# Other buffers for two scratch tiles, and two changes of order, in a kernel of two transformer blocks

## The chip, the cores and the metric

The kernel runs on one core of one Trainium2 chip. The metric is the device time of one execution in microseconds, the median of three runs. Engines are named as in the profile: PE is TensorE, ACT is ScalarE, DVE is VectorE, POOL is GpSimd, and SP is the engine whose queue issues nearly all DMAs.

## The reference, cut to what matters

One sequence of 512 tokens of width 1024 passes through two transformer blocks of float32 weights.

```python
# first block
h = rms_norm(x, ln_pre_mix); proj = h @ w_in          # 256 pool columns, q, k, v of 12 heads of 64
q, k = rope(q, pos), rope(k, pos)
mix = concat(multi_scale_pool(proj), dilated_attention(q, k, v)) @ w_out
x = x + rms_norm(mix, ln_post_mix)
f = (silu(h2 @ w_gate) * (h2 @ w_up)) @ w_down        # h2 = rms_norm(x, ...), inner width 2816
x = x + rms_norm(f, ln_post_ffn)
# second block
z = rms_norm_2(h, ln_mix) @ w_in                      # parts q1 q2 k1 k2 va | qf kf vf fg | qc kc vc
q1, q2, k1, k2, qf, kf, qc, kc = (rms_norm_2(each head, gain) for each part)
o_a = diff_attention(q1, q2, k1, k2, va, lam, ...)    # 4 heads: softmax(q1 k1) - lam * softmax(q2 k2)
o_b = forgetting_attention(qf, kf, vf, log_f)         # 6 heads, cumulated log of a forget gate as bias
o_c = chunk_attention(qc, kc, vc, rel_bias)           # 6 heads, relative bias
h = h + concat(o_a, o_b, o_c) @ w_out
h = h + conv_gated_mlp(rms_norm_2(h, ln_ffn), w_up, conv_w, conv_b, w_down)
h = h + (p @ w_ple_proj) * sigmoid(rms_norm_2(h, ln_ple) @ w_ple_gate)
```

## The kernel before

**Matmuls.** Every product with weights is made of three TensorE passes: hi times hi, hi times lo and lo times hi, where hi is a value rounded for TensorE and lo the rest. A projection with 256 output columns (`chunk`, L374 to L376) takes 96 matmuls: four token tiles, eight input slices, three passes. Two token tiles share a PSUM bank, so each projection has two halves, and a function `out_of` takes a half out of PSUM as soon as it is complete. The slabs of the output projections (`slab`, L188 to L190) have 512 columns and put 128 output features into one bank.

**Weights.** `wunit` (L151) requests 512 KB of weights by one DMA on SP (L159) into a landing buffer of the tag "raw", of which the pool `wts` holds four. ACT copies each half of it to a hi tile (L165), and DVE, or now and then POOL, subtracts to get the lo tile (L168). When both halves are converted the landing buffer is free. Hi and lo tiles have nine buffers each.

**Slots.** Other tiles come from tags with fixed counts (`SLOTS`: sixteen "h", six "z", eight "m" and so on). Buffers of a tag are handed out in the order in which the program asks for them, and a tile waits until the last readers of the buffer's tile before are done. PSUM has three banks for projections and head transposes, two for scores, two for transposed weights of the attention, and one for outputs.

**Order of the work.** The attention part of each block is written as a string of steps (`ORDER1`, `ORDER2`), which `play` calls one by one. Of block 2's letters these matter here: D makes the first two projections, P and a digit one more (all with a norm of each head); V and a letter one of the value projections VM, VA, VF and VC; T and a digit transposes a projection's result into heads (L318), evacuates them by ACT and DVE (L330 to L333) and moves halves between partitions by copies on SP (L420); S and two digits makes scores (L263, L264, then L267 and L113), W transposes the softmax (L285) and multiplies it with values (L293, L294); F is the decay of the forgetting heads (L976 and more copies on SP); O is an output slab made early from the heads that are done. A scheduler then turns the recorded program into one fixed order for each engine, which it may change against the string, where dependencies allow it.

**The four places of the change.** In block 1 `out_of` of `project` copies a projection into a z slot (L488), and the rotation uses a second z slot, `y` (POOL L493, L494, DVE L495 to L497). In block 2 `out_of` of `projected` copies the half into a z slot (ACT, L832), writes its square into a second one (ACT, L833), and DVE reduces the square to eight sums for each row (L835); Ln and Exp (both L113) and a few small steps on DVE make the factors that POOL applies. `ORDER2` has the steps D, VM, H, P3, T1, T0 at its start. `add_out` loops over the eight slabs of an output projection; for the first four of w_out2 (`short` is 4) only the part over the last two heads tiles is left, since the steps O made the rest.

Of the kernel before, what the change touches and what calls it, by code (L numbers as in the profile page):

```python
# [9 lines left out]
F32 = mybir.dt.float32  # L10
# [5 lines left out]
P = 128  # L16
S = 512
D = 1024
KD = D // P
# [4 lines left out]
WH = 524  # L24
# [10 lines left out]
    "W31 S40 V2 S41 T5 U0 w40 s50 U1 B W41 S51 W50 W51 "  # L35
)
ORDER2 = (
# [3 lines left out]
)  # L41
# [21 lines left out]
class Builder:  # L63
# [388 lines left out]
    def mix1(self):  # L452
        nc = self.nc
        io = self.io
        x, h = [], []
        early = self.units("w_qk1", 0)
        for k in range(KD):
            x.extend(self.load_x((k,)))
            h.append(self.split(x[k], self.col("ln_pre_mix", k), tag="h"))
            if k in (0, 4):  # L460
                early(k // 4)
        self.rest()
        rope = self.slot("m", F32, (P, 4, 96))
        nc.sync.dma_start(rope, io["rope"])
        nc.sync.dma_start(self.ident, io["ident"])
        acc = self.slot("m")
        for k in range(KD):
            self.square_acc(acc, x[k], k == 0, after=self.last)
        R = self.slot("m")
        rc = self.rstd_cols(acc)  # L470
        rot = self.slot("m", F32, (P, 4, 96))
        for t in range(4):
            nc.vector.tensor_scalar(rot[:, t], rope[:, t], rc[:, 2 * t:2 * t + 1], None, ALU.mult)
        tab = self.slot("m")
        nc.sync.dma_start(tab, io["tab_mult"])

        zs = {}
        ops = {}
        ps = {}
        outs = {}  # L480

        def project(i):
            zs[i] = []

            def out_of(t1, ps):
                t0 = t1 - 1
                z, y = self.slot("z"), self.slot("z")
                nc.scalar.activation(z, ps, AF.Copy)  # L488
                zv, yv = [a.rearrange("p (t h d) -> p t h d", t=2, d=64) for a in (z, y)]
                cs = rot[:, t0:t0 + 2, 0:64].unsqueeze(2).to_broadcast([P, 2, 4, 64])  # L490
                sn = rot[:, t0:t0 + 2, 64:96].unsqueeze(2).to_broadcast([P, 2, 4, 32])
                a, b = slice(0, 32), slice(32, 64)
                nc.gpsimd.tensor_tensor(yv[:, :, :, a], zv[:, :, :, b], sn, ALU.mult)  # L493
                nc.gpsimd.tensor_tensor(yv[:, :, :, b], zv[:, :, :, a], sn, ALU.mult)  # L494
                nc.vector.tensor_tensor(zv, zv, cs, ALU.mult)  # L495
                nc.vector.tensor_tensor(zv[:, :, :, a], zv[:, :, :, a], yv[:, :, :, a], ALU.subtract)
                nc.vector.tensor_tensor(zv[:, :, :, b], zv[:, :, :, b], yv[:, :, :, b], ALU.add)  # L497
                zs[i].append(z)
            self.chunk("w_qk1", int(i), h, 256, out_of, i == "0", early)

        def heads(i):
            ops[i] = self.to_heads(zs[i], -0.125, None)

        oT = [None] * 8
        vts = []

        def values(g):
            vt = self.v_tiles()
            vts.append(vt)
            self.chunk("w_v1", int(g), h, 256, lambda t, ps: self.put_v2(vt, t, ps, rc))  # L510

        def score(i, e, wide=False):
            ps[i + e] = self.scores(ops[i][int(e)], tab, wide)

        def weigh(i, e, wide=False):
            i, e, p = int(i), int(e), ps[i + e]
            if e == 0:
                outs[i] = self.slot("o")
            j = (2 * i + e) % 4
            self.weigh(p, [vts[i // 2][t][:, j, :] for t in range(4)], outs[i], e == 1, wide)  # L520
            if e == 1:
                oT[2 + i] = self.split(outs[i], tag="o")

        us = []
        get = self.units("w_u1")

        def pool_in(i):
            if i == "0":
                self.rstd_rows(acc, R)
            u = self.psum()  # L530
            self.slab(u, "w_u1", int(i), h, units=get)
            t = self.slot("z")
            nc.vector.tensor_tensor(t, u, R, ALU.mult)
            us.append(t)

        self.play(ORDER1, P=project, T=heads, V=values, S=score, W=weigh, U=pool_in,
                  B=lambda: self.pool_branch(us, oT))
        return self.post(oT, DONE1, "w_out", "ln_post_mix", "ln_pre_ffn", True)
# [249 lines left out]
    def mix2(self, h, rc):  # L788
# [30 lines left out]
        zs = {}  # L819
# [7 lines left out]
        def projected(i):  # L827
            out = zs[i] = []

            def out_of(t1, ps):  # L830
                z, sq = self.slot("z"), self.slot("z")
                nc.scalar.activation(z, ps, AF.Copy)  # L832
                nc.scalar.activation(sq, ps, AF.Square)  # L833
                st = self.small(8)
                nc.vector.tensor_reduce(st, sq.rearrange("p (h d) -> p h d", d=64), AX.X, ALU.add)  # L835
                four = lambda v: v[:, t1 - 1:t1 + 1].unsqueeze(2).to_broadcast([P, 2, 4])
                two = lambda v: v.rearrange("p (t h) -> p t h", h=4)
                nc.vector.tensor_tensor(two(st), two(st), four(r2), ALU.mult)
                y, w = self.small(8), self.small(8)
                self.act(y, st, AF.Ln, bias=self.eps, scale=1.0)  # L840
                self.act(y, y, AF.Exp, scale=-0.5)
                nc.vector.scalar_tensor_tensor(w, st, EPS, y, ALU.add, ALU.mult)
                nc.vector.scalar_tensor_tensor(w, w, -0.5, y, ALU.mult, ALU.mult)
                nc.vector.tensor_tensor(two(y), two(y), four(r1), ALU.mult)
                nc.vector.scalar_tensor_tensor(st, w, 1.5, y, ALU.add, ALU.mult)
                zv = z.rearrange("p (h d) -> p h d", d=64)
                nc.gpsimd.tensor_tensor(zv, zv, st.unsqueeze(2).to_broadcast([P, 8, 64]), ALU.mult)
                out.append(z)
            return out_of
# [88 lines left out]
        def early(m):  # L938
# [10 lines left out]
                  F=lambda: fr.extend(self.decay(gates)), G=self.ple)  # L949
# [45 lines left out]
    def add_out(self, a, wname, nname, order=None, tag="z", old=None, short=0):  # L995
        nc = self.nc
        get = self.units(wname)
        h = self.h_tiles()
        old = old or self.res
        getb = self.units(wname + "b")  # L1000
        for m in range(KD):
            ps = self.psum(True)
            hv = ((0, S),) if m < KD - 1 else ((0, 256), (256, S))
            if m < short:
                self.slab(ps, wname, m, a, order[KA2:], hv, getb)
            else:
                self.slab(ps, wname, m - short, a, order, hv, get)
            for c0, c1 in hv:
                c = slice(c0, c1)
                nc.vector.tensor_tensor(self.res[m][:, c], old[m][:, c], ps[:, c], ALU.add)  # L1010
                self.split(self.res[m], self.col(nname, m), *h[m], cols=c)
        return h, self.stats(True, tag)
# [196 lines left out]
```

## Time and profile before

| what | value |
|---|---|
| runs, us | 1325.31, 1321.66, 1320.98; median 1321.66 |
| profiled execution, us | 1321.43 |
| its span, us | 1319.6 |
| TensorE's mean granted clock | 0.998 of full speed |
| busy, us | PE 1287.4, DVE 926.1, ACT 713.9, POOL 141.2 |

The span is the part of the execution from the first instruction to the last. A busy time counts an engine's instructions, and TensorE's matmuls overlap, so that a start-to-start distance is read from a stretch without idle time, by its length and its count. The idle time that stands in brackets behind an instruction is that of its engine just before it, with the instruction that released it. The rows that are read closely stand in a section of their own below.

### The profile page before, as it was taken

The numbers are of one execution on the slowest core, as the hardware profiler recorded it, in microseconds if no ns is written. First come the engines' busy times: TensorE is split into PE (matmuls) and PEld (weight loads), VectorE is DVE, ScalarE is ACT, GpSimd is POOL, SyncE is SP. The second block draws the span as 40 slices with busy tenths as digits, with TensorE's granted clock in tenths as the row PEclk, the third lists the DMA queues.
The fourth block names the chain that finished last, engine by engine and source line by source line (L and its number), as shares of the span: only waits on it lengthen the run. The fifth ranks groups of instructions, "written<-read, shape, count | busy, mean of one in ns | idle before, by whom it ended". The sixth has DMA issues, their size and how long they took to land.

```text
span 1319.6 us, 21593 instructions
## 1 busy us (share of the span) xinstructions
PE 1287.4 (98%) x7990; PEld 1145.5 (87%) x7990; DVE 926.1 (70%) x1949; ACT 713.9 (54%) x1446; POOL 141.2 (11%) x185
## 2 busy tenths in 40 slices
PE   9899989999999999999999999899999999999998
PEld 9899878988999988898899999779888888888887
DVE  7777884899999833249788878657977777633354
ACT  6466645564666633247676777645544444522241
POOL 1223220000000000000232333420000000000000
PEclk9999999999999999999999999999999999999999
DMA  7421433421333442227335443323322222322211
GB/s 253 125 68 50 112 104 104 144 96 63 118 119 102 148 156 96 96 104 241 106 90 133 135 118 101 103 104 121 128 96 96 96 97 96 104 96 96 96 49 64
DMA packets 51114, 146.00 MB, mean 111 GB/s; under 512 B 6496, under 2 KB 7392, under 8 KB 51008
## 3 DMA queue, kind: packets, MB, share of 16 engines
q1 hardware_dynamic: 51008, 144.62, 33.8%
q8 instruction: 63, 1.03, 0.3%
q14 instruction: 43, 0.35, 0.1%
HBM read 124.47 MB, written 8.39 MB: 101 GB/s over the span
## 4 chain that ended last, share of the span: by engine, by line
PE 88%; DVE 6%; ACT 2%; issue 2%; DMA 1%; POOL 1%; SPq 0%; DVEq 0%; POOLq 0%; ACTq 0%
PE p L188 22%; PE p L190 22%; PE p L189 22%; PE p L374 5%; PE p L376 5%; PE p L375 5%; PE p L285 2%; PE p L294 1%; PE p L264 1%; PE p L263 1%; PE p L293 1%; DVE sp L267 1%; DVE wl L168 1%; PE p L318 1%; PE p L399 1%
## 5 line engine op out<-in xcount | busy, mean ns | idle before, releaser
L165 ACT ACTIVATE wh<-wr 128x512 fp32r<-128x512 f32 x357 | 222.0, 630 | 296.3 <-PE p L189 261.1
L168 DVE TENSOR_TENSOR wl<-wr,wh 128x512 fp32r<-128x512 f32 x345 | 246.5, 722 | 189.0 <-ACT wh L165 177.7
L188 PE MATMUL p<-sh,wh 128*128 128x512 f32 (+1 forms) x736 | 249.0, 343 | 2.4 <-DVE sv L416 2.4
L189 PE MATMUL p<-sh,wh 128*128 128x512 f32 (+1 forms) x736 | 250.6, 343 | 0.0
L190 PE MATMUL p<-sh,wl 128*128 128x512 f32 (+1 forms) x736 | 248.2, 343 | 0.0
L374 PE MATMUL p<-wh,sh 128*128 128x256 f32 (+1 forms) x672 | 190.2, 284 | 4.1 <-ACT sz L488 1.4
L375 PE MATMUL p<-wl,sh 128*128 128x256 f32 (+1 forms) x672 | 190.0, 283 | 0.2 <-DVE wl L168 0.2
L376 PE MATMUL p<-wh,sh 128*128 128x256 f32 (+1 forms) x672 | 189.4, 284 | 0.0
L188 PEld LDWEIGHTS p<-sh,wh 128*128 128x128 f32 x736 | 137.6, 188 | 19.9 <-issue 3.0
L189 PEld LDWEIGHTS p<-sh,wh 128*128 128x128 f32 x736 | 138.4, 188 | 17.6 <-issue 0.2
L190 PEld LDWEIGHTS p<-sh,wl 128*128 128x128 f32 x736 | 137.1, 188 | 17.9 <-issue 0.5
L374 PEld LDWEIGHTS p<-wh,sh 128*128 128x128 f32 x672 | 126.5, 189 | 7.2 <-ACT sz L488 1.6
L375 PEld LDWEIGHTS p<-wl,sh 128*128 128x128 f32 x672 | 126.8, 189 | 1.2 <-DVE wl L168 0.6
L376 PEld LDWEIGHTS p<-wh,sh 128*128 128x128 f32 x672 | 126.3, 189 | 0.7 <-DVE sh L181 0.3
L189 PE MATMUL p<-sk,wh 128*128 128x512 f32 (+1 forms) x306 | 106.9, 358 | 0.4 <-DVE sk L181 0.4
L190 PE MATMUL p<-sk,wl 128*128 128x512 f32 (+1 forms) x306 | 107.2, 358 | 0.0
L188 PE MATMUL p<-sk,wh 128*128 128x512 f32 (+1 forms) x306 | 99.7, 358 | 1.7 <-ACT sk L177 1.4
L113 ACT ACTIVATE sp<-sp,m 128x128 f32<-128x128 f32 (+3 forms) x128 | 71.5, 560 | 35.7 <-DVE m L267 31.7
L188 PE MATMUL p<-so,wh 128*128 128x512 f32 (+1 forms) x246 | 88.2, 362 | 1.4 <-DVE m L267 1.0
L190 PE MATMUL p<-so,wl 128*128 128x512 f32 (+1 forms) x246 | 88.6, 360 | 0.0
L275 POOL TENSOR_SCALAR sp<-sp,m 128x128 f32<-128x128 f32 (+1 forms) x112 | 69.2, 622 | 180.5 <-DVE m L271 149.2
L189 PE MATMUL p<-so,wh 128*128 128x512 f32 (+1 forms) x246 | 88.4, 359 | 0.0
(248 smaller groups left out, 2618.9 us busy)
## 6 DMA issues: line engine op xcount, KB each, us to landing
wr<-in_w_gu SPq DMA_DIRECT2D x88, 512.0 KB
wr<-in_w_down SPq DMA_DIRECT2D x44, 512.0 KB
wr<-in_w_qk SPq DMA_DIRECT2D x31, 512.0 KB
sk<-sk SPq DMA_DIRECT2D x88, 128.0 KB
wr<-in_w_out SPq DMA_DIRECT2D x12, 512.0 KB
sv<-in_x SPq DMA_DIRECT2D x16, 256.0 KB
wr<-in_w_ple_gate SPq DMA_DIRECT2D x8, 512.0 KB
wr<-in_w_v SPq DMA_DIRECT2D x6, 512.0 KB
```

The source lines that it names most:

```text
L113: i = self.nc.scalar.activation(out, in_, func, **k)
L165: nc.scalar.activation(hi[:, :w], c, AF.Copy)
L168: eng.tensor_tensor(lo[:, :w], c, hi[:, :w].bitcast(F32), ALU.subtract)
L188: mm(out, lhsT=ahi, rhs=bhi, start=start, stop=False, **more)
L189: mm(out, lhsT=ahi, rhs=blo, start=False, stop=False, **more)
L190: mm(out, lhsT=alo, rhs=bhi, start=False, stop=stop, **more)
L263: nc.tensor.matmul(ps[:, :n], lhsT=q1[:, c], rhs=k1[:, :n], start=True, stop=False)
L275: self.nc.gpsimd.tensor_scalar(p[:, :n], p[:, :n], m[:, 2:3], 1.0, ALU.mult, ALU.mult)
L285: ins = nc.tensor.transpose(pt[:, w:w + P], ps_list[qb][:, kb * P:kb * P + P], self.ident)
L374: mm(d, lhsT=h[k][0][:, a], rhs=hi[:, c], start=k == 0 and (o == 0 or not first), stop=False)
L375: mm(d, lhsT=h[k][0][:, a], rhs=lo[:, c], start=False, stop=False)
L376: mm(d, lhsT=h[k][1][:, a], rhs=hi[:, c], start=False, stop=k == 7 and (o > 0 or not first))
```

## The change

Four edits. Block 1's rotation scratch `y` no longer comes from the z slots: two m slots, allocated once, are used in turn. Block 2's squares no longer come from the z slots: each is written into a weight landing buffer, tag "raw", whose first 512 columns it uses. In `ORDER2` the step T1 stands ahead of P3 rather than behind it. In `add_out` slab number `short` (the first that is made over all eight heads tiles) is made first; where `short` is 0, as for w_down2, the order of the slabs is as it was.

```diff
--- before.py
+++ after.py
@@ -35,7 +35,7 @@
     "W31 S40 V2 S41 T5 U0 w40 s50 U1 B W41 S51 W50 W51 "
 )
 ORDER2 = (
-    "G0 G1 D VM H P3 T1 T0 S00 S01 F P2 T3 P4 T2 VA W00 T4 S10 W01 N0 P5 S11 W10 S20 W11 P6 N1 T5 VF "
+    "G0 G1 D VM H T1 P3 T0 S00 S01 F P2 T3 P4 T2 VA W00 T4 S10 W01 N0 P5 S11 W10 S20 W11 P6 N1 T5 VF "
     "S30 W20 W30 P8 S21 S31 T6 W31 W21 P7 S40 T8 VC T7 S60 S41 W40 P9 S50 T9 W60 S51 w41 S61 W50 S70 W51 "
     "S71 O0 W61 O2 O3 W70 O1 W71 "
 )
@@ -474,6 +474,8 @@
         tab = self.slot("m")
         nc.sync.dma_start(tab, io["tab_mult"])
 
+        turned = [self.slot("m") for _ in range(2)]
+
         zs = {}
         ops = {}
         ps = {}
@@ -484,7 +486,7 @@
 
             def out_of(t1, ps):
                 t0 = t1 - 1
-                z, y = self.slot("z"), self.slot("z")
+                z, y = self.slot("z"), turned[len(zs[i]) % 2]
                 nc.scalar.activation(z, ps, AF.Copy)
                 zv, yv = [a.rearrange("p (t h d) -> p t h d", t=2, d=64) for a in (z, y)]
                 cs = rot[:, t0:t0 + 2, 0:64].unsqueeze(2).to_broadcast([P, 2, 4, 64])
@@ -828,7 +830,8 @@
             out = zs[i] = []
 
             def out_of(t1, ps):
-                z, sq = self.slot("z"), self.slot("z")
+                z = self.slot("z")
+                sq = self.wp.tile([P, 2 * WH], F32, tag="raw", name=self.nm("wr"))[:, :S]
                 nc.scalar.activation(z, ps, AF.Copy)
                 nc.scalar.activation(sq, ps, AF.Square)
                 st = self.small(8)
@@ -998,7 +1001,7 @@
         h = self.h_tiles()
         old = old or self.res
         getb = self.units(wname + "b")
-        for m in range(KD):
+        for m in [short] + [m for m in range(KD) if m != short]:
             ps = self.psum(True)
             hv = ((0, S),) if m < KD - 1 else ((0, 256), (256, S))
             if m < short:
```

Lines of the changed kernel are two higher behind the first hunk in `mix1`, and three higher behind the one in `projected`: the evacuation is L835, the Square L836, the decay L979.

What the scheduler makes of it is seen at three places. The first is ACT at the end of D, in the kernel before: evacuations and Squares (L832, L833) of the first halves, and conversions of weights (L165); wh_7581 is the last of VM's, wh_7687 the first of P3's.

```order
L832 ACTIVATE sz_7386<-p_7248 128x512
L833 ACTIVATE sz_7387<-p_7248 128x512
L165 ACTIVATE wh_7581<-wr_7575 128x524
L832 ACTIVATE sz_7402<-p_7249 128x512
L833 ACTIVATE sz_7403<-p_7249 128x512
L832 ACTIVATE sz_7516<-p_7418 128x512
L165 ACTIVATE wh_7687<-wr_7685 128x512
L165 ACTIVATE wh_7691<-wr_7685 128x512
```

And in the changed kernel, from the last evacuation of D on, where wh_7545 is the first conversion of VM's weights:

```order
L835 ACTIVATE sz_7522<-p_7409 128x512
L836 ACTIVATE wr_7523<-p_7409 128x512
L113 ACTIVATE m_7399<-m_7399 128x8
L113 ACTIVATE m_7513<-m_7510,eps 128x8
L113 ACTIVATE m_7513<-m_7513 128x8
L165 ACTIVATE wh_7545<-wr_7543 128x524
L165 ACTIVATE wh_7549<-wr_7543 128x524
```

In the kernel before VM's last and P3's first conversions stand between the evacuations of D's first three halves. In the changed one VM's first conversion stands behind the last Square of D and three small operations.

The second place is SP. Before, where wr_8122 is the second half of P2's weights, wr_8278 and wr_8300 are P4's, wr_8460 and wr_8482 VA's, wr_8797 and wr_8819 P5's, and sk_7845 belongs to the heads of the first transposes:

```order
L159 DMA wr_8122<-in_w_qk 128x1024
L159 DMA wr_8278<-in_w_qk 128x1024
L159 DMA wr_8300<-in_w_qk 128x1024
L159 DMA wr_8460<-in_w_va 128x1024
L159 DMA wr_8482<-in_w_va 128x1024
L159 DMA wr_8797<-in_w_qk 128x1024
L159 DMA wr_8819<-in_w_qk 128x1024
L420 DMA sk_7845<-sk_7845 64x512
```

After, where sm_8071 belongs to the copies of the decay, sk_8250 to sk_8260 to the heads of T3, and wr_8268 and wr_8290 are P4's weights:

```order
L420 DMA sm_8071<-sm_8056 2x512
L420 DMA sm_8071<-sm_8055 2x512
L420 DMA sm_8071<-sm_8056 2x512
L420 DMA sk_8250<-sk_8250 64x512
L420 DMA sk_8251<-sk_8251 64x512
L159 DMA wr_8268<-in_w_qk 128x1024
L159 DMA wr_8290<-in_w_qk 128x1024
L420 DMA sk_8259<-sk_8259 64x512
L420 DMA sk_8260<-sk_8260 64x512
```

P4's request stood ahead of all copies of heads; it now stands behind those of the decay and of the first half of T3. P6's request (wr_9128, not shown) likewise moved from a place ahead of the decay's second group of copies to one behind all sixteen copies of T4 and a table.

The third place is TensorE between P3 and P2. Before, P3's last matmul, T1's transposes, the decay's matmuls and the first of T0's transposes:

```order
L376 MATMUL p_7769<-wh_7713,sh_6787 128x256
L318 MATMUL p_7834<-ident,sz_7532 128x128 x2
L318 MATMUL p_7834<-ident,sz_7402 128x128 x2
L318 MATMUL p_7835<-ident,sz_7532 128x128 x2
L318 MATMUL p_7835<-ident,sz_7402 128x128 x2
L976 MATMUL p_8057<-sm_8055,m_8053 6x512
L976 MATMUL p_8057<-sm_8055,m_8053 6x384
L976 MATMUL p_8057<-sm_8055,m_8053 6x256
L976 MATMUL p_8057<-sm_8055,m_8053 6x128
L318 MATMUL p_7862<-ident,sz_7516 128x128 x2
L318 MATMUL p_7862<-ident,sz_7386 128x128 x2
```

After, VM's last matmul, T1's transposes and P3's first matmuls:

```order
L376 MATMUL p_7646<-wh_7571,sh_6777 128x262
L318 MATMUL p_7674<-ident,sz_7522 128x128 x2
L318 MATMUL p_7674<-ident,sz_7392 128x128 x2
L318 MATMUL p_7675<-ident,sz_7522 128x128 x2
L318 MATMUL p_7675<-ident,sz_7392 128x128 x2
L374 MATMUL p_7702<-wh_7705,sh_6762 128x256
```

T1's transposes (of sz_7532 and sz_7402 before, sz_7522 and sz_7392 after) moved from behind P3 to ahead of it; behind P3 now come T0's and the decay, and P2's two halves start in turns.

## Rows read from the trace of the kernel before

**Rows 1.** The page: TensorE's busy time; the chain that ended last, by engine.

```profile
PE 1287.4 (98%) x7990; PEld 1145.5 (87%) x7990; DVE 926.1 (70%) x1949; ACT 713.9 (54%) x1446; POOL 141.2 (11%) x185
...
PE 88%; DVE 6%; ACT 2%; issue 2%; DMA 1%; POOL 1%; SPq 0%; DVEq 0%; POOLq 0%; ACTq 0%
```

**Rows 2.** Stretches: length, busy (x count) of PE PEld DVE ACT POOL, clock, DMA, GB/s.

```profile
600.00:626.20 26.20, 23.97 (x195) 22.96 (x194) 23.80 (x61) 17.95 (x43) 1.28 (x1) 1.00 0.69 236
626.20:637.70 11.50, 11.50 (x97) 11.50 (x96) 9.11 (x32) 6.39 (x17) 5.03 (x5) 1.00 0.15 47
648.90:656.00 7.10, 4.91 (x29) 2.70 (x28) 6.88 (x10) 6.96 (x14) 0.62 (x1) 1.00 0.70 204
680.00:700.00 20.00, 18.87 (x149) 17.68 (x149) 17.23 (x47) 13.13 (x30) 6.85 (x8) 1.00 0.34 93
700.00:800.00 100.00, 100.00 (x795) 96.75 (x794) 83.87 (x243) 72.91 (x179) 34.75 (x43) 1.00 0.47 130
```

**Rows 3.** Line L488 (ACT): what its engine waited for, and who waited for it.

```profile
  DVE sz L497: 6.2, 3
...
  PE p L374: 1.4, 1
```

**Rows 4.** TensorE in D: start, length, instruction, idle before it and its releaser.

```profile
613.15 0.39 PE L397 MATMUL p<-wh,sh 128*128 128x256 f32 x1 [0.42 <-ACT sh L180]
```

**Rows 5.** DVE at the same place.

```profile
612.73 0.71 DVE L168 TENSOR_TENSOR wl<-wr,wh 128x524 fp32r<-128x524 f32 x1 [0.85 <-ACT wh L165]
613.35 0.48 DVE L181 SCALAR_TENSOR_TENSOR sh<-sv,cols,sh 128x256 fp32r<-128x256 f32 x1
```

**Rows 6.** SP: issues of weights and copies, merged where adjacent (x count).

```profile
620.21 6.58 SPq L159 DMA_DIRECT2D wr<-in_w_qk  x3
...
667.19 2.57 SPq L159 DMA_DIRECT2D wr<-in_w_qk  x2
...
672.14 4.86 SPq L420 DMA_DIRECT2D sm<-sm  x8
...
711.69 4.60 SPq L420 DMA_DIRECT2D sk<-sk  x6
...
721.56 1.31 SPq L420 DMA_DIRECT2D sk<-sm  x2
```

**Rows 7.** ACT after half of P3, and a head evacuation.

```profile
643.25 0.60 ACT L832 ACTIVATE sz<-p 128x512 f32<-128x512 f32 x1 [2.51 <-PE p L376]
...
645.29 0.30 ACT L113 ACTIVATE m<-m,eps 128x8 f32<-128x8 f32 x1 [0.95 <-DVE m L838]
...
645.63 0.21 ACT L113 ACTIVATE m<-m 128x8 f32<-128x8 f32 x1
...
671.17 0.68 ACT L330 ACTIVATE sk<-p,gq 64x512 fp32r<-64x512 f32 x1
```

**Rows 8.** Line L835 (DVE): durations min/median/max in ns, first and last start.

```profile
L835 DVE TENSOR_REDUCE m<-sz x20: 660/679/686, 622.5 to 823.3; 128x8 f32<-128x512 f32 x20
```

**Rows 9.** An isolated request of weights on SP, and its first use on ACT.

```profile
20.07 2.14 SPq L159 DMA_DIRECT2D wr<-in_w_v  x2
...
23.52 0.63 ACT L165 ACTIVATE wh<-wr 128x512 fp32r<-128x512 f32 x1 [0.99 <-DMA wr<-in_w_v]
```

**Rows 10.** The page: the group of matmuls in which the output projection waits.

```profile
L188 PE MATMUL p<-sk,wh 128*128 128x512 f32 (+1 forms) x306 | 99.7, 358 | 1.7 <-ACT sk L177 1.4
```

**Rows 11.** TensorE at T1, T0 and P2.

```profile
653.90 0.63 PE L318 MATMUL p<-ident,sz 128*128 128x128 f32 x4 [1.32 <-DVE sk L331]
655.40 0.36 PE L374 MATMUL p<-wh,sh 128*128 128x256 f32 x1 [0.87 <-DVE sk L333]
```

**Rows 12.** Stretches around two gaps of TensorE, columns as in rows 2.

```profile
652.00:654.00 2.00, 0.68 (x5) 0.47 (x6) 1.94 (x5) 1.92 (x5) 0.00 (x0) 1.00 0.72 245
...
829.00:831.00 2.00, 0.33 (x2) 0.30 (x2) 0.68 (x5) 0.64 (x3) 1.98 (x3) 1.00 0.05 15
...
831.74:835.15 3.41, 3.25 (x14) 2.94 (x14) 2.04 (x6) 1.76 (x3) 2.83 (x5) 0.50 0.00 0
```

## The prediction

> **What bounds the kernel now.** I read the page first: TensorE is busy for 98% of the span and is 88% of the chain that ended last [rows 1]. Time can be won only where TensorE is not fed. The stretches say where that is. From 700 to 800 us, in the middle of block 2's attention, it has no idle at all, and one projection of 97 matmuls takes 11.50 us, which is 0.119 us for a matmul of 256 columns [rows 2]. The idle lies where the change works: the first two projections of block 2, D (600 to 626.2 us), lose 26.20 - 23.97 = 2.23 us, the head transposes T1 and T0 lose 7.10 - 4.91 = 2.19 us, and 680 to 700 us loses 1.13 us [rows 2]. The profiled execution took 1321.43 us, its span 1319.6 us and 1.8 us around it; the median of the runs is 0.23 us higher. I add my terms to 1321.43.
>
> **Block 1's rotation scratch.** ACT's evacuation of a projection (L488) stood still for 6.2 us in three cases, because the "z" slot that it wants is held by the rotation of an earlier projection (DVE L497); TensorE waited for it for 1.4 us [rows 3]. With y in two slots of its own, z slots come free sooner. The wait of TensorE goes: -1.4. Bounds: 0 if y's alternation now holds the next rotation instead (POOL, which writes y, is behind ACT only), and twice it, -2.8, if the other two of the three cases, which TensorE sat out with other work, had each pushed something behind them. I take -1.4, the row's own size.
>
> **Squares in a landing buffer: what goes.** In D TensorE waits five times for a part of an activation (L180 on ACT, L181 on DVE), the first time for 0.42 us [rows 4]; the window's loss of 2.23 is their sum. DVE also converts VM's weights there (L168, 524 columns wide as VM's alone are): one conversion starts at 612.73, and the activation's lo part behind it 0.62 us later [rows 5]. After the change VM's weights arrive only behind D, so four conversions of 0.62, 2.5 us, leave DVE there. That is more than the loss. I take -2.2; the bounds are 0 (the chain of D's own DVE work is then the bound) and -2.5.
>
> **Squares in a landing buffer: what comes.** The weight landing buffers "raw" are four, handed out in program order. Before, weights alone passed through them, so that P4's could be requested at 620.21 us and P6's at 667.19, a projection or more ahead of their use [rows 6]. Now each projection with a norm takes two of the buffers for its squares, between its own weights and those of the next. The next weights can be requested only after that point of the program, and their conversion on ACT (L165) stands behind the evacuation, Square, Ln and Exp of the projection before, as the first order piece shows for VM.
>
> The price for VM, step by step. In the rows of P3 the evacuation starts at 643.25 and Exp ends at 645.63 + 0.21 = 645.84, 2.6 us later, with the reduction (0.68, [rows 8]) between Square and Ln [rows 7]. Then come the first hi copy, 0.63 [rows 9], and the lo subtraction, 0.71 [rows 5]: 3.9 us from D's last matmul to VM's second matmul. Beside it TensorE has nothing that is ready, as VM follows at once. Before, VM started with no wait and ran 11.50 us of 11.50 [rows 2]. Term: +3.9; bounds 1.3 (the two conversions alone) and 3.9 + 3.45 (if the request, too, comes only then). The 3.45 is what a request takes: issued at 20.07, used by ACT at 23.52 [rows 9].
>
> P4's request now stands on SP behind the copies of T3's first heads (second order piece). After P2's last matmul come the eight transposes of T3 (twice 0.63, [rows 11]), two head evacuations of 0.68 [rows 7], one DVE part of about 0.7, and two copies of 0.61 (4.86 for eight, [rows 6]): 1.3 + 1.4 + 0.7 + 1.2 = 4.6 us. Then 3.45 to land, 0.63 and 0.71 to convert: 9.4 us. Beside it TensorE has, in the order, T3's transposes, fourteen score matmuls and eleven transposes of weights of the attention. At 0.12 to 0.23 us each I put these at 4.6. Left: +4.8; bounds 1.3 and 9.4.
>
> P6's request stands behind all sixteen copies of T4, which took from 711.69 to 721.56 + 1.31 = 722.87, 11.2 us [rows 6], and a table load of about 0.4. In the order the first of these copies waits for a score matmul that stands 36 projection matmuls and a few others, about 4.7 us, before P5's end. So the request comes 11.2 + 0.4 - 4.7 = 6.9 us after P5, and the first weights are ready 6.9 + 3.45 + 0.63 + 0.71 = 11.7 us after it. TensorE's own work there is about 5.2 (scores and transposes as above). Left: +6.5; bounds 1.3 and 11.7.
>
> VA, VF, P7 and VC have their weights landed in time, but the hi copies stand behind the same 2.6 us of ACT and the two conversions, 3.9 in all; some 1.5 to 2.4 us of transposes lie beside each. I take +2 each, +8 together; bounds 0 and 4 x 3.9. From P8 on the order on TensorE is nearly that of before, so I add nothing.
>
> The scores, transposes and weigh matmuls that move into these gaps leave the projections, where they stood between matmuls and waited now and then: the 1.13 us of 680 to 700 [rows 2] go, -1.1 (bounds 0 and -1.3).
>
> **T1 ahead of P3.** Before, T0's transposes waited 1.32 us for a PSUM bank that T1's heads freed, and P2's first matmul 0.87 us for one that T0's freed [rows 11]. With P3's 11.2 us between the two, T1's heads are long evacuated when T0 comes (third order piece): the 1.32 goes. The 0.87 stays, and P2 now wants two banks early, as its halves are interleaved: -1.0 with bounds +1.0 and -2.2. T1 itself follows VM at once, when its rows have been normalised for some 10 us.
>
> **Full slab first in the output projection.** TensorE waits there 1.4 us for the last heads (L177) [rows 10]. The last matmuls ahead of that wait are the same in both orders: only what is before them is permuted. 0, bounds -1.4 and +1.4. For w_down2 there is no short slab and nothing changes.
>
> **Sum.** -1.4 - 2.2 + 3.9 + 4.8 + 6.5 + 8.0 - 1.1 - 1.0 + 0 = +17.5, so 1338.9 us. I say 1338.5.
>
> The clock stands against even this. After a gap in which TensorE was busy 0.33 of 2.00 us (829 to 831 us) its granted clock fell to 0.50, the lower level of 1.2 GHz, for 3.41 us from 831.74; after 652 to 654, with 0.68 of 2.00 us busy, it stayed at 1.00 [rows 12]. Work worth 1.7 us at the full clock was done in these 3.41, so that one fall costs 1.7 us.
>
> The Trainium skill, page "TensorE: Matmul & The Clock Gate", section "HAM oscillation — how this bites in real kernels", has the rule: matmul groups with idle waits for data between them fall back to the low clock again and again. The trace agrees once and disagrees once [rows 12]; by the rule alone the three longest gaps would each cost a fall, and the time would be the 1343.6 us of the first rival.
>
> **Rivals.**
> 1. The gaps cost the clock too: VM, P4 and P6, the three longest waits, fall each, 3 x 1.7 = +5.1, 1343.6 us; with all seven waits 1350. For it: the gap of 829 to 831 did it. Against: attention work is sprinkled into most of the new gaps, as in 652 to 654.
> 2. Near zero: only the two conversions, 0.63 + 0.71 = 1.3, are exposed at each of seven late projections, 9.4, because TensorE finds scores and transposes for the rest. Minus the gains 1.4 + 2.2 + 1.1 + 1.0 = 5.7 that is +3.7, 1325.1. For it: the order interleaves two or three output tiles of the late projections, as one does when weights trickle in. Against: neither tile can start without the first hi copy.
> 3. Faster: the late weights are all hidden, and the gains of 5.7 remain: 1315.7. It decides as soon as the seven waits together stay under 1.7 us. For it: 512 KB land in 3.45 us [rows 9], a third of a projection's 11.50 [rows 2]. Against: the attention stages had no idle from 700 to 800 us [rows 2] just because weights were requested a projection ahead, and there is no lead any more.
>
> **Chances.** The sum as it stands 0.60, with its own range 1328 to 1347; the clock 0.15; near zero 0.13; faster 0.12. A measurement of this kernel tells about 0.3%, 4 us, from no change. So slower 0.75, same 0.13, faster 0.12. The range that should hold the time 8 times in 10 is 1320 to 1349: it takes in rival 2 and most of rival 1, and leaves out rival 3 and the far end of the clock.
>
> **What would show it.** In the profile after, TensorE should wait at the first matmuls (L374) of VM, P4, P6, VA, VF, P7 and VC for ACT's hi copies (L165), 2 to 6.5 us each, and the requests of these weights (L159) should start only behind the copies on SP; for P4 and P6 a landing DMA should end just before the copy. D should be about 24 us long with its DVE waits gone, and L488 should no longer wait for L497. Shorter waits than 1.3 us at these places, or weights that were requested in time, would make the prediction wrong, and so would new waits in P8 to P9, where I counted none.

## The result and the profile after

The changed kernel takes 1365.97 us (median of 4 runs, 1364.05 to 1367.27) against 1323.10 for the kernel before on the same chips: a ratio of 1.031, interval 1.029 to 1.034. Forecast were 1338.5 us, with 1349 as the upper end. The direction was right and the size was not: the change costs 42.9 us, two and a half times my sum.

The profiled execution took 1364.05 us, its span is 1362.3. The page after, the rows that answer to [rows 1], with the strip of TensorE's granted clock in 40 slices of 34 us:

```profile
PE 1308.0 (96%) x7990; PEld 1160.2 (85%) x7990; DVE 934.2 (69%) x1949; ACT 711.5 (52%) x1446; POOL 147.1 (11%) x185
...
PEclk9999999999999999998979999899999999999999
...
PE 86%; DVE 7%; ACT 3%; DMA 2%; issue 1%; SPq 0%; POOL 0%; DVEq 0%; ACTq 0%; POOLq 0%
```

The number of matmul records is the same, 7990. The span has grown by 42.7 us, but TensorE's idle time (span less busy) only from 32.2 to 54.3, by 22.1. The other 20.6 us are in the busy time: the same instructions took longer. The dips in the clock strip say why. Over windows of 1 us I summed TensorE's busy time times (1 - granted clock), the work lost to the lower clock level: 1.7 us in the kernel before, 19.6 after. So 17.9 of the 20.6 us are work done at that level. Of these, 1.7 us lie in block 1, behind a fall of the clock at 160 us, and 16.2 in block 2. What the other 2.7 us are is not shown.

This is not a matter of the one profiled execution: the four executions of the changed kernel have mean granted clocks of 0.980 to 0.982. Of 84 executions of the kernel before, taken beside the experiments, none is below 0.990, and their median is 0.995.

What TensorE waited for from 598 to 905 us after the change (line waited for, total us, times, longest):

```profile
PE p L374 <- ACT wh L165: 7.9, 5, 3.4
PE p L263 <- DVE m L267: 4.2, 7, 1.5
PE p L285 <- DVE st L178: 3.8, 2, 3.1
PE p L375 <- DVE wl L168: 3.0, 4, 1.6
PE p L294 <- DVE st L178: 2.9, 4, 2.0
PE p L285 <- DVE sp L891: 2.4, 2, 1.4
...
PE p L375 <- POOL wl L168: 2.0, 1, 2.0
```

Waits for hi and lo copies of weights (L165, L168) lead; the same stretch before had none. Attention work that now stands alone in the gaps waits for its softmax.

Stage by stage, from the last matmul of one projection to the last of the next (starts of the first and last matmul of each PSUM tile, read from the two traces to 0.1 us, so that a length or a difference can be off by that), the longer time is where the weights are late. The term of -1.1 for 680 to 700 us lies in P4 and VA and is not in the last column:

| stage | before | after | more | my term |
|---|---|---|---|---|
| up to D | 598.7 | 599.7 | +1.0 | -1.4 |
| D | 27.0 | 24.1 | -2.9 | -2.2 |
| VM | 11.6 | 19.0 | +7.4 | +3.9 |
| P3 and P2 | 31.0 | 32.2 | +1.2 | -1.0 |
| P4 | 15.6 | 26.0 | +10.4 | +4.8 |
| VA | 16.2 | 17.8 | +1.6 | +2 |
| P5 | 18.2 | 17.8 | -0.4 | 0 |
| P6 | 17.8 | 28.5 | +10.7 | +6.5 |
| VF | 15.2 | 16.9 | +1.7 | +2 |
| P8 | 18.0 | 16.0 | -2.0 | 0 |
| P7 | 15.8 | 22.9 | +7.1 | +2 |
| VC | 17.4 | 22.1 | +4.7 | +2 |
| P9's first half | 12.2 | 12.3 | +0.1 | 0 |
| from there to the end | 504.9 | 507.0 | +2.1 | 0 |

The +1.0 up to D is the fall at 160 us; TensorE's idle time up to there is 14.2 us in both.

Four of these stages in the trace after, each as the gap ahead of it and the projection itself (columns as in [rows 2]):

```profile
623.80:627.50 3.70, 0.33 (x4) 0.13 (x3) 1.77 (x7) 2.28 (x7) 1.34 (x2) 1.00 0.48 163
627.50:642.80 15.30, 14.56 (x95) 14.26 (x96) 9.73 (x23) 5.65 (x12) 5.20 (x4) 0.78 0.18 64
675.10:685.50 10.40, 6.69 (x36) 4.26 (x35) 10.21 (x33) 9.21 (x25) 1.87 (x3) 0.84 0.43 133
685.50:701.10 15.60, 14.00 (x96) 13.71 (x97) 8.71 (x27) 4.48 (x11) 5.38 (x5) 0.78 0.38 130
736.70:746.90 10.20, 7.45 (x40) 4.95 (x38) 8.91 (x37) 8.05 (x24) 2.79 (x4) 1.00 0.72 202
746.90:765.20 18.30, 18.30 (x120) 17.47 (x121) 13.66 (x39) 8.88 (x23) 7.89 (x8) 0.81 0.28 92
798.20:803.50 5.30, 3.85 (x25) 2.96 (x23) 4.75 (x17) 5.15 (x14) 0.85 (x2) 1.00 0.03 8
803.50:821.00 17.50, 17.03 (x124) 16.27 (x125) 9.07 (x30) 8.66 (x24) 7.39 (x9) 0.90 0.72 193
```

And P6 before, the gap and the projection:

```profile
718.50:720.50 2.00, 2.00 (x16) 1.47 (x14) 1.97 (x4) 1.98 (x5) 1.63 (x2) 1.00 0.74 160
720.50:736.20 15.70, 15.70 (x128) 15.44 (x125) 15.28 (x57) 11.43 (x32) 5.45 (x7) 1.00 0.39 116
```

The reader is to see two things. The gaps are there: 3.70, 10.40, 10.20 and 5.30 us. And the projection behind each runs at a mean clock of 0.78 to 0.90, so P6, with 120 matmuls in 18.30 us, took longer than before with 128 in 15.70. It was never idle in that time.

The requests are where the order put them. SP after, around P4's and P6's requests, and ACT's first use of P4's weights, rows that answer to [rows 6]:

```profile
678.58 2.45 SPq L420 DMA_DIRECT2D sk<-sk  x2
681.08 1.06 SPq L159 DMA_DIRECT2D wr<-in_w_qk  x2
...
740.73 1.31 SPq L420 DMA_DIRECT2D sk<-sm  x2
742.09 0.44 SPq L101 DMA_DIRECT2D sm<-in_tab_causal  x1
742.56 0.91 SPq L159 DMA_DIRECT2D wr<-in_w_qk  x2
```

```profile
684.79 1.15 ACT L165 ACTIVATE wh<-wr 128x512 fp32r<-128x512 f32 x2 [0.77 <-DMA wr<-in_w_qk]
```

P4's request came at 681.08, 6.0 us after P2's last matmul (675.05), P6's at 742.56, 6.0 us after P5's (736.55). Expected were 4.6 and 6.9. Landing took 684.79 - 681.08 = 3.71 us.

### The profile page after: what moved, and what is told of

Same layout as the page of the kernel before. It is cut to its first block, busy times and chain, and to the rows that moved or that the text cites. A ratio compares the mean times of both kernels' runs of the same rounds, so it can differ in the third digit from the quotient of the medians.

```text
span 1362.3 us, 21564 instructions
## 1 busy us (share of the span) xinstructions
PE 1308.0 (96%) x7990; PEld 1160.2 (85%) x7990; DVE 934.2 (69%) x1949; ACT 711.5 (52%) x1446; POOL 147.1 (11%) x185
## 4 chain that ended last, share of the span: by engine, by line
PE 86%; DVE 7%; ACT 3%; DMA 2%; issue 1%; SPq 0%; POOL 0%; DVEq 0%; ACTq 0%; POOLq 0%
PE p L188 21%; PE p L189 21%; PE p L190 21%; PE p L375 6%; PE p L376 6%; PE p L374 5%; DVE wl L168 1%; PE p L285 1%; PE p L294 1%; PE p L263 1%; PE p L293 1%; PE p L264 1%; DMA sk<-sk 1%; DVE sp L267 1%; DVE sk L331 1%
## 5 line engine op out<-in xcount | busy, mean ns | idle before, releaser
L165 ACT ACTIVATE wh<-wr 128x512 fp32r<-128x512 f32 x357 | 218.6, 629 | 287.0 <-PE p L189 263.1
L168 DVE TENSOR_TENSOR wl<-wr,wh 128x512 fp32r<-128x512 f32 x345 | 245.6, 722 | 176.1 <-ACT wh L165 163.8
L374 PE MATMUL p<-wh,sh 128*128 128x256 f32 (+1 forms) x672 | 194.3, 294 | 10.5 <-ACT wh L165 7.9
L375 PE MATMUL p<-wl,sh 128*128 128x256 f32 (+1 forms) x672 | 195.6, 293 | 5.0 <-DVE wl L168 3.0
L376 PE MATMUL p<-wh,sh 128*128 128x256 f32 (+1 forms) x672 | 192.6, 289 | 0.0
L188 PEld LDWEIGHTS p<-sh,wh 128*128 128x128 f32 x736 | 137.9, 189 | 20.5 <-issue 3.2
L190 PEld LDWEIGHTS p<-sh,wl 128*128 128x128 f32 x736 | 137.4, 189 | 17.9 <-issue 0.2
L374 PEld LDWEIGHTS p<-wh,sh 128*128 128x128 f32 x672 | 131.4, 197 | 14.1 <-ACT wh L165 9.9
L375 PEld LDWEIGHTS p<-wl,sh 128*128 128x128 f32 x672 | 132.2, 197 | 7.7 <-DVE wl L168 5.0
L376 PEld LDWEIGHTS p<-wh,sh 128*128 128x128 f32 x672 | 131.6, 197 | 0.8 <-DVE sh L181 0.3
```

The lines of the kernel that those rows point to most:

```text
L165: nc.scalar.activation(hi[:, :w], c, AF.Copy)
L168: eng.tensor_tensor(lo[:, :w], c, hi[:, :w].bitcast(F32), ALU.subtract)
L188: mm(out, lhsT=ahi, rhs=bhi, start=start, stop=False, **more)
L190: mm(out, lhsT=alo, rhs=bhi, start=False, stop=stop, **more)
L374: mm(d, lhsT=h[k][0][:, a], rhs=hi[:, c], start=k == 0 and (o == 0 or not first), stop=False)
L375: mm(d, lhsT=h[k][0][:, a], rhs=lo[:, c], start=False, stop=False)
```

## The experiments

The main theory after the result: squares in the ring of landing buffers push the requests of weights behind them, the late weights open gaps, and TensorE's clock falls in or behind the gaps, so that each late projection is paid twice. Times are medians beside the kernel before on the same chips; a ratio's interval is in brackets.

**One edit alone: the squares.**

```diff
-                z, sq = self.slot("z"), self.slot("z")
+                z = self.slot("z")
+                sq = self.wp.tile([P, 2 * WH], F32, tag="raw", name=self.nm("wr"))[:, :S]
```

> The kernel before with one edit: block 2's squares in the weight landing buffers. Theory (the squares in the ring of landing buffers cost it all): 1355 to 1370 us, slower than before by 35 to 45. Rival (the order of T1 and P3, or the slab order, carries a good part): under 1350. Rival (the edits only hurt together): within 6 us of before.

Measured: 1362.03 us against 1324.17, 1.028 (1.026 to 1.030). This one edit alone carries most of the loss, 37.9 of 42.9 us. It falls on other stages than in the changed kernel, though: VM is 7.5 us longer, P4 5.8, VA 9.0, P6 only 3.4, P7 7.4. The gap ahead of P6 is shorter here, and P6 runs at the full clock:

```profile
741.50:747.50 6.00, 4.93 (x31) 3.57 (x30) 4.53 (x17) 5.95 (x16) 0.19 (x1) 1.00 0.70 261
747.50:762.80 15.30, 15.30 (x123) 14.83 (x122) 13.78 (x46) 10.26 (x28) 7.79 (x9) 1.00 0.30 105
```

Which stage pays thus changes with the rest of the kernel more than the sum does.

**All but that edit** (the same lines the other way round in the changed kernel).

> The changed kernel with the squares back in z slots: rotation scratch, T1 ahead of P3 and full slab first remain. Theory: within 0.5% of before, 1315 to 1328, since the losses all came from the landing buffers; my terms of -1.4 for the rotation, -1.0 for T1 and 0 for the slab would give 1320. Rival: 1335 or more, if one of these three carries a part of the loss.

Measured: 1322.42 us, 0.9985 (0.9973 to 0.9997). The other three edits together are worth about 2 us. By the stages of its trace P3 and P2 together are 1.4 us shorter (+2.1 and -3.5), VA is 0.4 longer, and the others from D on are equal within 0.1. The part up to D is 2.7 us longer; there the clock fell twice, at 64 and at 197 us, which it did not in the profiled execution of the kernel before. So T1 ahead of P3 gives 1.4 us, of which VA gives 0.4 back: the 1.0 that I had put it at. The trace with that edit alone has the same -1.4 and +0.4.

**Squares in one buffer of their own.**

```diff
-                sq = self.wp.tile([P, 2 * WH], F32, tag="raw", name=self.nm("wr"))[:, :S]
+                sq = self.wp.tile([P, S], F32, tag="sq", name=self.nm("sq"), bufs=1)
-SLOTS = dict(h=16, o=14, k=16, z=6, v=8, p=8, t=6, m=8)
+SLOTS = dict(h=16, o=14, k=16, z=5, v=8, p=8, t=6, m=8)
```

> The changed kernel with the squares in one buffer of their own, neither z nor landing buffer; to pay for it there are five z slots, not six. Theory: with the weights' ring free of squares the 43 us are gone, 1319 to 1329. Rival (it is the scheduler's new order that costs, whatever buffers the squares use): 1340 or more.

Measured: 1324.99 us, 0.9999 (0.9986 to 1.0013). Taking the squares out of z is harmless; sharing the ring with weights is what costs.

**Squares in the ring, requests ahead of them.** The next projection's two units are asked for at the top of `out_of`, before its first square.

```diff
+        def ahead(i):
+            if i == "0":
+                i = "1"
+            if i in follows and follows[i] not in ready:
+                name, ci = follows[i]
+                g = self.units(name)
+                g(2 * ci)
+                g(2 * ci + 1)
+                ready[name, ci] = g
...
             def out_of(t1, ps):
+                ahead(i)
                 z = self.slot("z")
```

> The changed kernel, squares still in the landing buffers, but the program asks for the next projection's 1 MB of weights ahead of a projection's first square, so that their requests no longer stand behind the squares. Theory (it is the place of the request behind the squares that costs): most of the 43 us come back, 1320 to 1340, and TensorE's clock stays high in block 2. Rival (squares that occupy two to four of the four landing buffers leave too few for weights, wherever the request stands): 1350 or more.

Measured: 1327.83 us, 1.0024 (1.0011 to 1.0037). Of 43 us some 39 came back, with the squares where the change put them. I had expected the clock to stay high in block 2; it fell there twice, at 812 and 836 us, against once in the kernel before, and P9's first half is 5.2 us longer, 1.6 of it by the clock. P6 in its trace is at full clock and without idle time, 15.30 us long:

```profile
720.70:722.80 2.10, 2.10 (x16) 1.57 (x16) 0.70 (x2) 1.58 (x3) 0.12 (x1) 1.00 0.96 204
722.80:738.10 15.30, 15.30 (x124) 14.99 (x123) 14.76 (x48) 10.97 (x30) 5.15 (x5) 1.00 0.63 208
```

Four landing buffers are therefore enough for weights and squares, but for these 0.24%; the place of the request in the program's order decides.

**One late request: the squares of P5 alone.**

```diff
+                if i in "5":
+                    sq = self.wp.tile([P, 2 * WH], F32, tag="raw", name=self.nm("wr"))[:, :S]
+                else:
+                    sq = self.slot("z")
```

> The kernel before, with the squares of P5 alone in landing buffers, so that only P6's requests move: behind the sixteen copies of T4 and a table. Theory: P6 waits as in the changed kernel, where the stretch from P5's end to P6's end was 10.7 us longer; 1331 to 1337 us, 8 to 12 slower than before. By my recorded term alone, without the clock, +6.5: 1329. Rival (one late request is absorbed by the slack of the others): within 3 us of before.

Measured: 1337.00 us (1329.78 to 1339.24), 1.0105 (1.0074 to 1.0135). Of the stages in the table P6's is 11.0 us longer, as in the changed kernel (10.7), P9's first half 5.2 longer, 1.7 of it by a fall of the clock at 815 us. VF, P8 and VC are 1.1, 1.8 and 1.0 shorter, the part behind P9's first half 3.2, and the others are within 0.7 of before. Gap and projection:

```profile
717.70:727.70 10.00, 7.53 (x39) 5.02 (x38) 8.59 (x36) 8.05 (x24) 2.79 (x4) 1.00 0.70 193
727.70:746.50 18.80, 17.17 (x119) 16.08 (x120) 16.45 (x42) 12.45 (x31) 8.90 (x9) 0.91 0.51 181
```

**The same with the gap filled.** Between P5 and P6 stand 24 more matmuls of ones, issued after P5's last:

```diff
+            if i == "5":
+                fill(24)
```

> P5's squares alone in landing buffers, as in the run on P5 alone, and 24 extra matmuls of ones (about 5 us of work, results unused) between P5 and P6, where TensorE waits about 10 us for P6's weights. In the run on P5 alone the stretch from P5's end to P6's end was 28.8 us against 17.8 before. Theory (the clock falls in the sparse gap and P6 then runs at half clock): with the gap filled the stretch is 25 to 27 us although 5 us of work are added, there is no stretch at half clock in P6, and the median is 1328 to 1334. Rival (the wait for the weights is all): the stretch is 29 to 34 us, the median 1337 or more.

Measured: 1331.31 us, 1.0044 (1.0026 to 1.0062), an interval below that of the kernel without the filling. Gap and projection:

```profile
723.90:735.50 11.60, 11.06 (x80) 9.30 (x79) 9.09 (x31) 6.72 (x18) 3.27 (x4) 1.00 0.75 228
735.50:750.60 15.10, 15.10 (x124) 14.87 (x123) 15.10 (x41) 12.30 (x32) 6.74 (x8) 1.00 0.51 176
```

The profile has two records for each of the added matmuls, 48 in all. With added work the kernel became faster. The gap is 1.6 us longer, P6 is 3.7 us shorter (18.80 to 15.10) and at full clock, so that the two together are 2.1 us shorter. Of P6's 3.7 us, 1.7 are the fall of the clock (0.09 x 18.80), and 1.6 are idle time that stood inside P6. That a sparse gap costs time beyond itself is so shown, for the 1.7 us of the clock.

The median fell by more, by 5.7 us, and the filling is not the only difference: the scheduler also ordered TensorE's work from P6 to P9 in another way, and P9's first half is 17.4 us in one trace and 12.2, as in the kernel before, in the other. The clocks of all executions still point to the clock. The four without filling have mean granted clocks of 0.997, 0.992, 0.992 and 0.989, the first of them profiled and the fastest; the seven with filling have 0.993 to 1.000. (1 - clock) times the span bounds the work lost from above, as it counts idle time too; its median is 10.7 us without filling and 5.3 with it. Taken off each time, it leaves medians of 1325.4 and 1325.8 us, closer than the rounding of the clocks to 0.001 lets one tell (0.7 us). In which stages the executions without a profile lost it is not known.

**All gaps filled.** Twenty such matmuls behind each of D, P2, P4, P5, P6, P8 and P7 of the changed kernel:

```diff
+FILL = (2, 4, 5, 6, 8, 7)
+FILLS = 20
...
+            if int(i) in FILL:
+                fill(FILLS)
```

> The changed kernel with 20 extra matmuls of ones (128 columns, float32, results unused) behind each of D, P2, P4, P5, P6, P8 and P7, so that TensorE is busy for about 4 us of each new gap; nothing else is taken away, and the weights come as late as before. Theory (about 18 of the 43 us are work done at half clock after the gaps): the stretches at half clock in block 2 shrink from 44 us to under 20, and the time falls by 3 to 12 us in spite of about 30 us of added work, to 1354 to 1363. Rival (the clock's fall costs nothing by itself, because the weights are what is waited for anyway): the same time or longer, 1366 to 1380, even where the clock stays high.

Measured: 1360.86 us, 1.0280 (1.0256 to 1.0303); the changed kernel has 1.0289 to 1.0335, so the totals alone do not separate the two. The mean granted clocks do: 0.990 to 0.994 with filling, 0.980 to 0.982 without. By the stages of the trace VM, P4, P6 and P7 are 7.4, 10.4, 10.7 and 7.1 us longer than before without filling, and 5.0, 7.6, 8.4 and 4.0 with it, though each has about 4.5 us more to do. VA, VF and VC are 1.6, 1.7 and 4.7 longer without and 2.0, 3.3 and 13.1 with it. So all seven together cost the same, 43.6 and 43.4 us, with some 31 us of added work in them. The profiled execution was the slowest of the four (1365.95 us). VM after its filled gap, at full clock:

```profile
624.90:629.40 4.50, 4.50 (x43) 4.50 (x42) 2.65 (x9) 3.17 (x8) 1.56 (x2) 1.00 0.58 206
629.40:641.60 12.20, 11.98 (x98) 11.77 (x98) 8.78 (x22) 4.78 (x11) 4.75 (x3) 1.00 0.15 52
```

The sum of busy time times (1 - clock) fell from 19.6 to 11.3 us, not to nothing. Of under 20 us that I had expected at half clock in block 2, three falls made 20.5, against 44.4 without filling. VC's work grew by 2.6 us more than was added there, so attention work was displaced into it.

**The squares of D alone** (as for P5, with `"01"`).

> The kernel before, with the squares of D alone in landing buffers, so that VM's weights come late and their conversions leave D. Theory: VM's stretch grows by 7 us as in the changed kernel and D's shrinks by 2: +4 to +7, 1327 to 1331. By my recorded terms, +3.9 - 2.2 = +1.7: 1325. Rival (the time that VM loses is found again in the stages behind it): within 1.5 us of before.

Measured: 1327.56 us, 1.0023 (1.0008 to 1.0038). D is 2.8 us shorter, VM 6.2 longer: both halves of the term show. The gap ahead of VM and VM itself:

```profile
625.90:629.50 3.60, 0.23 (x2) 0.03 (x1) 1.75 (x7) 2.27 (x7) 1.24 (x2) 1.00 0.48 157
629.50:643.80 14.30, 13.25 (x96) 13.05 (x97) 11.80 (x25) 8.03 (x16) 5.65 (x5) 0.88 0.64 217
```

3.37 us of idle time where I had 3.9; the rest is the clock of 0.88 and the second unit of weights.

**The other three edits, each alone.** Rotation scratch:

```diff
-                z, y = self.slot("z"), self.slot("z")
+                z, y = self.slot("z"), turned[len(zs[i]) % 2]
```

> The kernel before with one edit: block 1's rotation scratch in two m slots. My recorded term: -1.4, 1322 to 1323 against 1324. Rival (y's own two slots bring a new wait, or two m slots fewer do): 0 to +2.

Measured: 1321.54, 0.9985 (0.9968 to 1.0002). Order:

```diff
-    "G0 G1 D VM H P3 T1 T0 S00
+    "G0 G1 D VM H T1 P3 T0 S00
```

> The kernel before with one edit: T1 ahead of P3 in block 2. My recorded term: -1.0, about 1323 against 1324. Rival (T1's transposes now wait for normalised rows, or P2 for its banks): 0 to +2.

Measured: 1322.13, 0.9985 (0.9969 to 1.0001). Full slab first:

```diff
-        for m in range(KD):
+        for m in [short] + [m for m in range(KD) if m != short]:
```

> The kernel before with one edit: the full slab of the output projection first. My recorded term is 0: within 1 us of before, the wait of 1.4 us for the last heads still there. Rival: that wait goes, -1.5.

Measured: 1325.52, 1.0005 (0.9992 to 1.0018). None of the three is told from no change by itself. The traces say more. With the rotation scratch apart, TensorE's wait for L488 is gone from block 1, but the scores wait for copies of heads instead (e5, waits from 0 to 210 us):

```profile
PE p L263 <- DMA sk<-sk: 2.1, 2, 1.7
```

In the kernel before that row was small:

```profile
PE p L263 <- DMA sk<-sk: 0.3, 1, 0.3
```

So TensorE's idle time up to D fell by only 0.8 us with this edit alone (14.2 to 13.4), not by the 1.4 of [rows 3], and in the changed kernel not at all. And the slab's wait is where it was, in the trace with that edit alone:

```profile
PE p L188 <- ACT sk L177: 1.4, 1, 1.4
```

**VM's conversions on POOL**, an attempt to have D's gain without VM's loss, on the kernel with all edits but the squares:

```diff
             if n == "M":
+                self.share = 1
                 self.chunk("w_vm", 0, h, 262, mid)
+                self.share = 0
```

> Rotation scratch, T1 ahead of P3 and full slab first, the squares in z slots, and the four lo subtractions of VM's weights on POOL rather than DVE. With the squares in landing buffers D lost its DVE waits and became 2.8 us shorter, but VM became 6 to 7 us later. Theory: VM's conversions are what hold D, so that POOL, idle there, gives the 2 to 2.8 us without the price: 1319 to 1321, where the kernel without this took 1322.4. Rival (D is held by its own DVE chain, or VM waits for POOL, which takes 1.3 us for each): 1322 or more.

Measured: 1323.93, 0.9997 (0.9985 to 1.0009). D did not become shorter but 2.7 us longer, with waits of up to 1.5 us for the same lo parts:

```profile
601.60:631.30 29.70, 26.69 (x200) 26.24 (x199) 24.34 (x59) 19.08 (x44) 7.84 (x5) 0.89 0.68 219
```

```profile
PE p L399 <- DVE sh L181: 3.0, 2, 1.5
```

The clock fell within D in this execution, and that accounts for the whole 2.7 us (0.11 x 29.70 = 3.3, its idle time counted in); the idle time is 3.0 us against 2.2 before. POOL took 1.3 to 1.8 us for each of the four conversions, DVE had taken 0.71 [rows 5]. The rival held, as the median is above 1322. That D lost its waits in the changed kernel is measured; whether it was DVE's four conversions that caused them stays open, since this trace, with its fall, does not decide it. Of all versions only the one without the squares is told from the kernel before as faster, by some 2 us.

## Why the prediction failed, step by step

**The mechanism of the waits was right.** Squares in the landing buffers put the requests behind them; TensorE waits at VM, P4, P6 and the rest for L165 and L168; the run with requests ahead of the squares takes it all away but 0.24%. The times of the requests came out within 1.4 us (6.0 us after the projection before in both cases, forecast 4.6 and 6.9), VM's gap at 3.7 against 3.9, P6's at 10.2 against 11.7.

**The step that failed is the clock.** The prediction set the clock apart as a rival with a chance of 0.15, "the three longest waits, fall each, 3 x 1.7 = +5.1". The sum had nothing for it; it measured 17.9 us, 16.2 of them in block 2. Both factors were too small. In the profiled execution the clock fell seven times in block 2, and four of these falls lasted 6.8 to 10.2 us, not 3.41 (by the same windows of 1 us). The last of the seven, behind P9, has its like in the kernel before, the one of [rows 12]; six are new. VM's 15.30 us with their mean of 0.78 show one of them: 0.22 x 15.30 / 0.5 = 6.7 us at half speed. And I held against it that "attention work is sprinkled into most of the new gaps, as in 652 to 654". That was the wrong row to lean on: in the gap ahead of P6 TensorE was busy for 7.45 of 10.20 us, the longest single idle time there was 0.97 us (ahead of a transpose of L285 at 746.22), and still the clock fell as P6 began (0.81 over P6). The fall behind 829 to 831 [rows 12] was the better guide. The rule of the Trainium skill (page "TensorE: Matmul & The Clock Gate", section "HAM oscillation — how this bites in real kernels") speaks of idle waits between groups of matmuls. The trace agrees for VM, whose gap was idle, and goes beyond it for P6.

**The idle sum was nearly right, its places were not.** My terms for waits and gains add up to +17.5; idle time grew by 22.1. Of these, 12.9 are waits for copies of weights (7.9 for hi, 3.0 and 2.0 for lo); the rest is, on balance, attention work that waits for its own softmax in the gaps (L263, L285 and L294 in the rows above). That it waits because it has lost the projection that covered it is argued, not shown by a run. P4 and P6 had 3.7 and 2.8 us idle ahead of them, less than the 4.8 and 6.5 that I gave them, since more attention work went there than I had counted. The prediction's rule for P8 and later, "so I add nothing", held for the stages up to P9 and missed 2.1 us behind them. That the two sums lie so close is in part luck: P6's stage had 2.8 us of new idle time for a term of 6.5, while VA, VF, P7 and VC together had 9.4 for 8.0, and the part behind P9 3.0 for nothing. The -1.1 for 680 to 700 us did not come; VA's stage had 2.9 us idle, 1.1 before.

**D, -2.2:** right, -2.9 with the slow first matmuls behind each wait. **VM, +3.9:** right for the gap, +7.4 in all with the clock. **VA and VF, +2 each:** +1.6 and +1.7, VA's by luck: 1.7 us of new idle time and 1.6 of half clock, less 1.7 of work that went elsewhere. **P7 and VC, +2 each:** +7.1 and +4.7, gaps of 5.3 and 5 us and the clock at 0.90 in P7. **T1 ahead of P3, -1.0:** right, -1.4 and 0.4 given back in VA (from the traces without the squares). **Rotation, -1.4:** the wait went and another took most of its place; the alternative that I had kept for it named POOL, it was the copies of heads on SP. **Slab, 0:** right.

The range was worked out from the bounds of the terms, and no term for work done at half speed was in it; that is why it missed by 17 us.

## What to carry to other kernels

Where a ring of buffers is handed out in program order, what else goes through it decides when the next load may be requested: ask for the load ahead of the tenant, or give the tenant its own buffer; the size of the ring was not the limit here. Where TensorE is busy all the time, price a new gap as its idle time plus the work behind it at half clock: here the second half was nearly as large as the first (17.9 and 22.1 us). Where a gap can't be closed, matmuls of no use in it can hold the clock up. In one gap of 10 us they came with 5.7 us less, the order behind it changed too; in all seven gaps at once a gain in time was not told from none.

## What was not expected of the hardware

The clock fell behind gaps that were not idle: ahead of P6 TensorE was busy for 7.45 of 10.20 us in the changed kernel and for 7.53 of 10.00 with P5's squares alone, and fell to half in both; behind the filled gap, 11.06 of 11.60 us, it stayed. It stayed, too, behind the 6.00 us with 4.93 busy in the kernel with the squares alone. And the clock's fall is not the same in each execution of the same instructions. Block 1 has the same order on TensorE in the kernel before and in the one with D's squares alone, yet the two profiled executions differ there (before, then the other):

```profile
158.00:165.00 7.00, 5.10 (x22) 4.18 (x23) 6.88 (x17) 4.42 (x10) 2.17 (x4) 1.00 0.46 129
195.00:201.00 6.00, 5.82 (x28) 4.88 (x29) 2.44 (x5) 1.30 (x4) 0.00 (x0) 1.00 0.19 48
```

```profile
158.00:165.00 7.00, 5.06 (x16) 4.11 (x17) 6.08 (x16) 4.45 (x10) 2.17 (x4) 0.76 0.49 131
195.00:201.00 6.00, 4.87 (x15) 3.74 (x16) 3.16 (x6) 1.62 (x4) 0.00 (x0) 0.72 0.39 130
```

Up to D the second is 3.0 us later for it. So a difference of 3 us between two single executions need not come from an edit. The executions without a profile say the same by their mean granted clocks. 29 of the kernel before, on the same chips as the run with D's squares, took 1319.3 to 1327.5 us at clocks from 1.000 down to 0.992; with (1 - clock) times the span taken off they lie between 1316.0 and 1320.4. The 9.5 us between the executions with P5's squares are of this kind: with the same taken off, 1324.5 to 1327.6 us are left.
